# Moving a quarter of a gate's modulation from the branch merge into the linear-attention heads

## The chip, the cores and the metric

The kernel runs on one core of a Trainium2 chip. The metric is the device time of one execution in microseconds (us); the time of a kernel is the median of its runs. Five engines work side by side, each through its own instruction queue and strictly in the order of that queue: TensorE (PE in the profile; PEld is its weight load), VectorE (DVE), ScalarE (ACT), GpSimd (POOL) and SyncE (SP), which only starts transfers. An instruction that has to wait holds up everything behind it on its engine.

## The reference, cut to what matters

One layer of a diffusion backbone: 512 latent tokens and 256 context tokens, 1024 channels, float32. The conditioning vector `c` makes six modulation rows of 1024 numbers, and the one this change is about is `gt2`, the gate of the second residual:

```python
mod = jax.nn.silu(c) @ w_ada[layer] + b_ada[layer]          # w_ada: 1024 x 6144
sh1, sc1, gt1, sh2, sc2, gt2 = jnp.split(mod[:, None, :], 6, axis=-1)
h = modulate(rms_norm(x_lat, norm1_g), sh1, sc1)
# token sub-layer: latent attention (8 heads) and gated linear attention (4 heads), then
g_mla, g_gla = jnp.split(sigmoid(gate_logits), 2, axis=-1)
mix = (g_mla * br_mla + g_gla * br_gla) @ w_out
x_lat = x_lat + gt1 * mix
h = modulate(rms_norm(x_lat, norm2_g), sh2, sc2)
val, gate = split(h @ w_up)                                  # 2 x 2816 channels
x_lat = x_lat + gt2 * ((gelu(conv3x3(gate)) * val) @ w_down)
return rms_norm(x_lat, final_g)
```

`gt2` depends only on `c` and on 4 MB of `w_ada`, so it can be made at any time before it is first used, at the end of the second sub-layer. The same holds of `gt1`, `sh2` and `sc2` with their own columns of `w_ada`.

## The kernel before, in words

Every large product is done as three products in a rounded format (fp32r): each float32 operand is split into a high part and a low remainder, and hi·hi, hi·lo and lo·hi are summed in PSUM. For weights, ACT casts the high part (`whi`, or `s` where it goes into the large pool), and POOL or DVE subtracts it from the raw tile for the low part (`wlo`, or `s`). So each 512 KB of weights costs one SP transfer, one ACT cast and one subtraction before PE can use it. Raw tiles have three buffers, and SP starts the next transfer when the subtraction has freed one.

The stages, with their place in the span of the profiled execution: input normalisation and latents (0 to about 85 us), latent attention (to about 205), four heads of gated linear attention (`states`, `output`, `decay`, `apply`, `to_tokens`, called in the loop over `h` in lines 1316 to 1340; to about 409), the branch merge (loop over `j` in lines 1383 to 1425; 409 to 475), the output projection `w_out_norm` (475 to 526), the up projection with the convolution (to about 788), the down projection and the final norm.

**The heads.** In the pass over head `h`, the decay factors of head `h + 1` are made (`decay`, line 1137): ACT takes exponentials, DVE takes running sums, first for the context (tiles `C`), then for the latents (tiles `T`). Then half the merge gates of the other branch (`merge_mla`) and the next keys and queries are projected, `apply` multiplies them by the decay factors on DVE, and `to_tokens` turns the result on PE. Heads follow each other with a period of 45 us in the trace.

**The merge.** For each of eight blocks `j` of 128 channels PE makes a gate (`gb`, 24 matmuls) and a branch projection (`bg`, 12 matmuls); ACT makes the sigmoid of the gate (three instructions on tile `sg`); DVE multiplies by `bg` (`sg<-pb,sg`), adds the other branch (`sg<-sg,s`); ACT casts the high part (`s<-sg`), DVE subtracts the low part (`s<-sg,s`). These are the left operands of the output projection. Beside this, blocks 0 to 3 make `gt1` (`mod_part`, eight multiply-adds on DVE each into a PSUM tile, `p<-xn,csilu,p`), blocks 1, 2, 3 and 5 load and split four of the eight row blocks of `w_out`, and blocks 5 and 6 make two parts of `gt2`. In block 6 ACT copies the sums of `gt1` (`xn<-p`, the high part) and DVE subtracts (`xn<-p,xn`, the low part); PE then sums both over the partitions (`p<-xn,one_r`). After the merge the last four row blocks of `w_out` are cast on ACT (`s<-raw`), and their low parts go to POOL (blocks 4 and 6) and DVE (5 and 7).

**A part of `gt2`.** `gate_part(j, pool)` (line 1098) makes 256 of its 1024 columns: SP loads two tiles `wa` of 512 KB (two buffers), and DVE runs eight multiply-adds of 128x256 into tile `gt2` (`gt<-wa,csilu,gt`), four for each load. Until it is summed over the partitions, in the up projection, `gt2` is used by nobody. Before the change parts 0 and 1 are made in the pass over the last head and parts 2 and 3 in blocks 5 and 6 of the merge.

**The last weights.** The hidden channels of the last four blocks are not in the pairs of the down projection; their weights (`last`, four tiles of `w_down`) are multiplied by `gt2` on DVE and split (lines 1629 to 1637). The code asks for one of them after each of the pairs 1 to 4.

**What sets the order.** A scheduler in the build orders each engine's queue from a simulated timeline; the order of the code is a priority, `tc.issue_after(x)` keeps an instruction behind `x` in that simulated order, and only true dependences become waits on the chip. So DVE runs what the scheduler expected to be ready, and waits if on the chip it isn't. Nearly all instructions are recorded through one helper, so the profile gives lines 89 and 90 for them; the tiles tell them apart.

Of the kernel before, what the change touches and what calls it, by code (L numbers as in the profile page):

```python
# [13 lines left out]
ALU = mybir.AluOpType  # L14
# [58 lines left out]
def block_kernel(ctx: ExitStack, tc: tile.TileContext, p, out):  # L73
# [61 lines left out]
    def tt(eng, out_, a, b, op):  # L135
        return eng.tensor_tensor(out=out_, in0=a, in1=b, op=op)
# [4 lines left out]
    def split(hi, lo, src, eng=None):  # L141

        A.copy(hi, src)
        sub(eng or G, lo, src, f(hi))
# [962 lines left out]
    with tc.tile_pool(name="egl", bufs=1) as eg:  # L1107
# [208 lines left out]
        for h in range(GH):  # L1316
            St = states(h, dec)
            on = output(h, dec, Q, St)
            if h + 1 < GH:
                dec = decay(h + 1)  # L1320
                merge_mla(2 * h)
                kq = proj_kq(h + 1)
                with tc.issue_after(key_end[0].ins):
                    mod_end()
            else:
                merge_mla(2 * h)
                mod_end()
                mod_begin(S4f)
                with tc.issue_after(load[0].ins):
                    gate_part(0, eg)  # L1330
                merge_mla(2 * h + 1)
                with tc.issue_after(load[0].ins):
                    gate_part(1, eg)
            gate_out(h, on, gr)
            if h + 1 < GH:
                Q = apply(kq, dec)
                gr = gate(h + 1)
                to_tokens(dec, Q)
                mod_begin(S4f)
                merge_mla(2 * h + 1)  # L1340

    behind.clear()

# [29 lines left out]
    with tc.tile_pool(name="emg", bufs=1) as em_:  # L1373
        def merge_weights(j):
            return (split_w(load_cols(w_in, CGB + j * 128)), split_w(load_cols(w_brg, j * 128, k1=4), 512))

        def mraw():
            return tl(em_, [128, 1024], F32, "xn", 3)


        gsum = p2()
        ahead = merge_weights(0)
        for j in range(8):
            wgb, wbg = ahead
            gb = pb()
            proj(wgb, gb)
            if j + 1 < 8:
                ahead = merge_weights(j + 1)
            bg = pb()
            for k in range(4):  # L1390
                bg_ = mm3(bg, k3(wbg[0], 4, 128)[:, k, :], k3(wbg[1], 4, 128)[:, k, :], yT[k][:, 0, :], yT[k][:, 1, :], k == 0,
                    k == 3)
            sg = tl(em_, [128, 512], F32, "sg", 2)
            si = sigmoid(sg, gb)
            tt(V, sg, bg, sg, ALU.mult)
            tt(V, sg, sg, m1[j // 2][:, j % 2, :], ALU.add)
            mg[j] = S4([128, 2, 512])
            split(mg[j][:, 0, :], mg[j][:, 1, :], sg, V)
            ahead_ = load[0].ins
            if j in (1, 2, 3, 5):  # L1400
                load_wo(len(wo), mraw)
            if j == 0:
                mod_end()
            with tc.issue_after(ahead_):
                if j < 4:
                    mod_part(2048 + j * 256, gsum[:, j * 256:j * 256 + 256], mraw)
                elif j == 4:
                    mod_begin(mraw, p2()[:, 0:256])
            if j == 6:
                m_, gh, gl = mp_tile(), *[tl(em_, [128, 1024], F32R, "xn", 3) for _ in range(2)]  # L1410
                with tc.issue_after(si.ins):
                    A.copy(m_, begun[7])
                    A.copy(gh, gsum)
                sub(V, gl, gsum, f(gh))
            elif j == 7:
                with tc.issue_after(bg_.ins):
                    mod_fin(7, m_)
                    gp = p2()
                    for half in range(2):
                        hs = slice(half * 512, (half + 1) * 512)  # L1420
                        total(gp[:, hs], gh[:, hs], gl[:, hs])
                        tt(V, gt1[:, hs], gt1[:, hs], gp[:, hs], ALU.add)
            if j in (5, 6):
                with tc.issue_after(load[0].ins):
                    gate_part(j - 3, em_)
        for k in range(4, 8):
            load_wo(k)
        h2h = [S4([128, 2, 512]) for _ in range(4)]
        h2l = [S4([128, 2, 512]) for _ in range(4)]
        def w_out_norm(t):  # L1430
            cs = slice(t * 128, (t + 1) * 128)
            mp = p2()
            for k in range(8):
                for half in range(2):
                    hs = slice(half * 512, (half + 1) * 512)
                    mm3(mp[:, hs], mg[k][:, 0, cs], mg[k][:, 1, cs], wo[k][0][:, hs], wo[k][1][:, hs], k == 0, k == 7)
            xn = mraw()
            for half in range(2):
                hs = slice(half * 512, (half + 1) * 512)
                tt(V, xn[:, hs], mp[:, hs], gt1[:, hs], ALU.mult)  # L1440
                tt(V, x2[t][:, hs], x2[t][:, hs], xn[:, hs], ALU.add)
            s2 = sm(1, "s2")
            A.activation(xn, x2[t], AF.Square, accum_out=s2)
            A.dma_start(out=x2_[t], in_=x2[t])
            r2 = rstd_exp(s2, 1, 1.0 / D)
            V.tensor_scalar(out=xn, in0=x2[t], scalar1=r2, scalar2=None, op0=ALU.mult)
            return xn

        def transposed(t, xn):
            cs = slice(t * 128, (t + 1) * 128)  # L1450
            for kk in range(2):
                tp = pb()
                for k in range(4):
                    PE.transpose(tp[:, k * 128:(k + 1) * 128], xn[:, (4 * kk + k) * 128:(4 * kk + k + 1) * 128], ident)
                ht = tl(em_, [128, 4, 128], F32, "ht2", 2)
                for k in range(4):
                    kt = 4 * kk + k
                    V.tensor_scalar(out=ht[:, k, :], in0=tp[:, k * 128:(k + 1) * 128], scalar1=modsc2[:, kt:kt + 1],
                                    scalar2=modsh2[:, kt:kt + 1], op0=ALU.mult, op1=ALU.add)
                for k in range(2):  # L1460
                    split(h2h[2 * kk + k][:, :, cs], h2l[2 * kk + k][:, :, cs], ht[:, 2 * k:2 * k + 2, :], V)


        n0 = w_out_norm(0)
        n1 = w_out_norm(1)
        transposed(0, n0)
        n0 = w_out_norm(2)
        transposed(1, n1)
        n1 = w_out_norm(3)
        w0 = [up_weights(i) for i in range(2)]  # L1470
        z0 = p2()
        ps0 = [(z0[:, 0:512], z0[:, 512:1024]), (pb(), pb())]
        up_mm(w0[0], ps0[0], 0, 256)
        transposed(2, n0)
        up_mm(w0[1], ps0[1], 0, 256)
        transposed(3, n1)
        w0.append([])
        for c0 in (FF + 256, 256):
            h_, l_ = S4([128, 1024]), S4([128, 1024])
            split(h_, l_, load_cols(w_up, c0))  # L1480
            w0[2].append((h_, l_))
        z0 = p2()
        ps0.append((z0[:, 0:512], z0[:, 512:1024]))
        up_mm(w0[2], ps0[2], 0, 256)
        for i in range(3):
            up_mm(w0[i], ps0[i], 256, 512)
# [6 lines left out]
    with tc.tile_pool(name="eff", bufs=1) as ef:  # L1493
# [122 lines left out]
        for n in range(NP):  # L1616
            r = raw_()
            SY.dma_start(out=r[:, 0:512], in_=w_down[:, 2 * n, 0:512])
            SY.dma_start(out=r[:, 512:1024], in_=sums_[n][:, 1536:2048])
            wa = split_w(r, eng=G if n < 2 else V)  # L1620
            r = raw_()
            SY.dma_start(out=r, in_=sums_[n][:, 0:1024])
            wb = split_w(r, eng=G if n < 2 else V)
            a, z = n == 0, n == NP - 1
            product(p1, first[n], 0, wa, 0, a, z)
            product(p6, first[n], 768, wa, 512, a, z)
            product(p7, first[n], 512, wb, 512, a, z)
            product(p5, first[n], 256, wb, 0, a, z)
            if n == 0:
                for k in range(NF - NL, NF):  # L1630
                    last.append(S4f())
                    load[0] = SY.dma_start(out=last[-1], in_=w_down[:, k, :])
            elif n < 5:
                with tc.issue_after(done[0].ins):
                    tt(V, last[n - 1], last[n - 1], gt2, ALU.mult)
                    wl_.append((S4([128, 1024]), S4([128, 1024])))
                    split(*wl_[-1], last[n - 1], V)
            if n == NP - 3:
                bw.append(back_weights(0))
        u1, u2, u7, c22 = halves(S4f()), halves(S4f()), halves(S4f()), halves(S4f())  # L1640
# [143 lines left out]
```

## Time and profile before

| what | before |
|---|---|
| time, median of 3 runs | 889.96 us (887.29 to 890.98) |
| time of the profiled execution | 888.12 us |
| its span, from first to last instruction | 885.9 us |
| granted PE clock, mean | 0.998 |
| PE busy in the four heads and the merge, 228 to 474 us | without a wait over 0.2 us |
| period of heads 1 to 3 | 44.96, 44.96, 45.02 us |
| merge: time of one block of 36 matmuls on PE | 8.16 us |
| DMA busy share, 455 to 461 us / 478 to 486 us | 1.02 / 0.01 |
| DVE busy, 455 to 474.6 us | 17.75 of 19.6 us |

Rows of the timeline give the start in us, the duration in us (from the first start to the last end where equal neighbours are merged), engine, line, operation, tile written <- tiles read, shape and number; in square brackets the idle time of the engine before the row and what ended it. Waits are listed as "engine tile line <- what it waited for: us in total, times, longest".

### The profile page before, as it was taken

The numbers are of one execution on the slowest core, as the hardware profiler recorded it, in microseconds if no ns is written. First come the engines' busy times: TensorE is split into PE (matmuls) and PEld (weight loads), VectorE is DVE, ScalarE is ACT, GpSimd is POOL, SyncE is SP. The second block draws the span as 40 slices with busy tenths as digits, with TensorE's granted clock in tenths as the row PEclk, the third lists the DMA queues.
The fourth block names the chain that finished last, engine by engine and source line by source line (L and its number), as shares of the span: only waits on it lengthen the run. The fifth ranks groups of instructions, "written<-read, shape, count | busy, mean of one in ns | idle before, by whom it ended". The sixth has DMA issues, their size and how long they took to land.

```text
span 885.9 us, 12813 instructions
## 1 busy us (share of the span) xinstructions
PE 866.9 (98%) x4794; PEld 737.0 (83%) x4794; DVE 647.1 (73%) x1049; ACT 412.6 (47%) x666; POOL 383.8 (43%) x258
## 2 busy tenths in 40 slices
PE   7999999999999999999998999999999999999996
PEld 6788899888888888888886889888888888878885
DVE  5477788875978686986678584986677666787856
ACT  4355766773454545444544332433334333365414
POOL 2512355450534342433653521777767776500004
PEclk9999999999999999999999999999999999999999
DMA  9970001217414242637982730656556755578602
GB/s 293 319 182 1 1 4 33 73 33 206 107 37 131 61 131 60 187 87 227 280 264 96 231 102 15 225 170 198 176 168 191 211 174 182 170 276 271 213 13 95
DMA packets 141648, 130.53 MB, mean 147 GB/s; under 512 B 7947, under 2 KB 122995, under 8 KB 141586
## 3 DMA queue, kind: packets, MB, share of 16 engines
q1 hardware_dynamic: 140354, 126.67, 46.9%
q10 hardware_dynamic: 832, 2.40, 0.7%
q8 instruction: 37, 0.61, 0.3%
q0 software_dynamic: 400, 0.65, 0.3%
q14 instruction: 25, 0.20, 0.1%
HBM read 115.87 MB, written 13.63 MB: 146 GB/s over the span
## 4 chain that ended last, share of the span: by engine, by line
PE 81%; DMA 7%; issue 4%; DVE 4%; POOL 2%; ACT 2%; SPq 0%; POOLq 0%; DVEq 0%; ACTq 0%
PE pb L90 41%; PE p L90 20%; PE pb L89 14%; PE p L89 6%; DMA raw<-in_w_ada_dram 3%; DMA raw<-in_w_br_gla_dram 2%; POOL wlo L90 1%; POOL s L90 1%; DVE s L90 1%; DMA s<-in_w_down_dram 1%; DMA xn<-in_w_ada_dram 1%; ACT P L90 1%; DVE mx L90 1%; DVE kT L90 0%; DMA xn<-in_w_out_dram 0%
## 5 line engine op out<-in xcount | busy, mean ns | idle before, releaser
L90 POOL TENSOR_TENSOR wlo<-raw,whi 128x1024 fp32r<-128x1024 f32 (+1 forms) x91 | 210.0, 2315 | 219.4 <-ACT whi L90 188.9
L90 PE MATMUL pb<-s,whi 128*128 128x512 f32 (+1 forms) x906 | 271.3, 382 | 0.0
L90 PEld LDWEIGHTS pb<-s,whi 128*128 128x128 f32 x906 | 167.3, 188 | 32.3
L90 PE MATMUL pb<-s,wlo 128*128 128x512 f32 (+1 forms) x453 | 172.7, 381 | 0.0
L90 ACT CAST whi<-raw 128x1024 fp32r<-128x1024 f32 (+1 forms) x106 | 102.9, 975 | 120.1 <-PE pb L90 47.4
L90 DVE SCALAR_TENSOR_TENSOR ac<-pb,cwT,ac 128x441 f32<-128x441 f32 (+2 forms) x160 | 110.9, 694 | 13.5 <-ACT ac L90 9.2
L89 PE MATMUL pb<-s,whi 128*128 128x512 f32 x320 | 101.2, 394 | 0.0
L90 PEld LDWEIGHTS pb<-s,wlo 128*128 128x128 f32 x453 | 85.2, 188 | 16.3
L90 PE MATMUL p<-s,s 128*128 128x512 f32 (+1 forms) x398 | 84.3, 364 | 2.4 <-POOL s L90 1.9
L90 PEld LDWEIGHTS p<-s,s 128*128 128x128 f32 x398 | 66.9, 189 | 15.1 <-POOL s L90 2.2
L89 PEld LDWEIGHTS pb<-s,whi 128*128 128x128 f32 x320 | 59.3, 188 | 11.5
L89 PE MATMUL pb<-s,wlo 128*128 128x512 f32 x160 | 62.8, 392 | 0.0
L90 PE MATMUL p<-whi,s 128*128 128x512 f32 x168 | 55.8, 393 | 0.0
L90 PE MATMUL pb<-whi,s 128*128 128x512 f32 x164 | 53.2, 390 | 0.0
L90 POOL TENSOR_TENSOR s<-s,edge 128x512 f32<-128x512 f32 x7 | 10.5, 1508 | 93.8 <-ACT s L90 93.8
L90 ACT ACTIVATE ac<-ac 128x512 f32<-128x512 f32 x22 | 13.9, 632 | 75.9 <-DVE ac L90 75.9
L90 PE MATMUL pb<-s,s 128*32 128x128 f32 (+2 forms) x340 | 46.1, 319 | 0.2 <-DVE rv L90 0.2
L90 DVE TENSOR_TENSOR pl<-pb,ph 128x512 fp32r<-128x512 f32 x48 | 33.0, 687 | 13.0 <-ACT ph L90 12.5
L90 PE MATMUL p<-kT,s 128*128 128x512 f32 (+1 forms) x192 | 41.2, 350 | 0.9 <-ACT P L90 0.9
L90 PEld LDWEIGHTS pb<-s,s 128*128 128x128 f32 (+1 forms) x340 | 36.1, 159 | 6.1 <-issue 0.7
L90 PE MATMUL p<-s,whi 128*128 128x256 f32 (+1 forms) x156 | 38.6, 338 | 0.0
L90 ACT CAST ph<-pb 128x512 fp32r<-128x512 f32 x48 | 28.2, 587 | 20.7 <-PE pb L90 20.5
(274 smaller groups left out, 1672.2 us busy)
## 6 DMA issues: line engine op xcount, KB each, us to landing
raw<-in_w_up_dram SPq DMA_DIRECT2D x44, 512.0 KB, 5.1
raw<-in_w_in_dram SPq DMA_DIRECT2D x28, 512.0 KB, 4.3
rawd<-in_w_down_dram SPq DMA_DIRECT2D x22, 512.0 KB, 5.2
s<-in_w_ada_dram SPq DMA_DIRECT2D x20, 512.0 KB, 6.8
ws<-rawd SPq DMA_DIRECT2D x18, 512.0 KB, 5.7
raw<-in_w_ada_dram SPq DMA_DIRECT2D x10, 512.0 KB, 7.5
xn<-in_w_ada_dram SPq DMA_DIRECT2D x10, 512.0 KB, 5.1
wa<-in_w_ada_dram SPq DMA_DIRECT2D x8, 512.0 KB, 5.7
```

Source lines behind the costliest of these rows:

```text
L89: return fn(*args, **kw)
L90: ins = fn(*args, **kw)
```

## The change

Parts of `gt2` change their place, and the code asks for the scaling of the last weights after other pairs. Nothing is computed differently.

```diff
             else:
                 merge_mla(2 * h)
                 mod_end()
                 mod_begin(S4f)
                 with tc.issue_after(load[0].ins):
-                    gate_part(0, eg)
+                    gate_part(1, eg)
                 merge_mla(2 * h + 1)
                 with tc.issue_after(load[0].ins):
-                    gate_part(1, eg)
+                    gate_part(2, eg)
             gate_out(h, on, gr)
             if h + 1 < GH:
...
                 mod_begin(S4f)
                 merge_mla(2 * h + 1)
+                if h == 1:
+                    with tc.issue_after(load[0].ins):
+                        gate_part(0, eg)
...
-            if j in (5, 6):
+            if j == 6:
                 with tc.issue_after(load[0].ins):
-                    gate_part(j - 3, em_)
+                    gate_part(3, em_)
...
-            elif n < 5:
+            elif n in (1, 2, 4, 5):
+                r = last[len(wl_)]
                 with tc.issue_after(done[0].ins):
-                    tt(V, last[n - 1], last[n - 1], gt2, ALU.mult)
+                    tt(V, r, r, gt2, ALU.mult)
                     wl_.append((S4([128, 1024]), S4([128, 1024])))
-                    split(*wl_[-1], last[n - 1], V)
+                    split(*wl_[-1], r, V)
```

What the scheduler makes of it, at three places. The first is DVE in the pass over head 1, where the decay factors for head 2 are made (`C` context, `T` latents); the changed kernel has:

```order
L90 TENSOR_TENSOR C_521_3170<-C_521_3170,C_520_3169 128x512
L90 SCALAR_TENSOR_TENSOR gt_404_2389<-wa_3492,csilu_78,gt_404_2389 128x256
L90 SCALAR_TENSOR_TENSOR C_520_3169<-ones_74,C_521_3170 128x256 x2
L90 SCALAR_TENSOR_TENSOR gt_404_2389<-wa_3492,csilu_78,gt_404_2389 128x256
L90 TENSOR_SCALAR C_521_3170<-C_520_3169 128x256 x2
L90 SCALAR_TENSOR_TENSOR gt_404_2389<-wa_3492,csilu_78,gt_404_2389 128x256 x2
L90 TENSOR_SCALAR T_519_3168<-p_515_3164,pcol_72 128x512
L90 SCALAR_TENSOR_TENSOR gt_404_2389<-wa_3498,csilu_78,gt_404_2389 128x256 x3
L90 TENSOR_SCALAR T_519_3168<-p_515_3164,pcol_72 128x512
L90 SCALAR_TENSOR_TENSOR gt_404_2389<-wa_3498,csilu_78,gt_404_2389 128x256
L90 TENSOR_REDUCE so_3152<-w_510_3150 128x4
```

The eight `gt` rows are new there and stand between rows that were neighbours before; the first of each four waits for its `wa` load. On SP the two `wa` loads stand right behind the load of `w_br_mla` for that pass. On ACT one exponential of `C` has moved behind the first `T<-p`. PE and POOL keep their order.

The second place is DVE in blocks 5 to 7 of the merge. Before, the sums of part 2 (`wa_4606`, `wa_4612`) and part 3 (`wa_4683`, `wa_4689`) stood between the rows of blocks 5 (`sg_4591`) and 6 (`sg_4668`):

```order
L90 SCALAR_TENSOR_TENSOR gt_404_2389<-wa_4606,csilu_78,gt_404_2389 128x256 x3
L90 SCALAR_TENSOR_TENSOR gt_404_2389<-wa_4612,csilu_78,gt_404_2389 128x256 x4
L90 TENSOR_TENSOR sg_4591<-pb_4578,sg_4591 128x512
L90 SCALAR_TENSOR_TENSOR gt_404_2389<-wa_4683,csilu_78,gt_404_2389 128x256
L90 TENSOR_TENSOR sg_4591<-sg_4591,s_594_3657 128x512
L90 SCALAR_TENSOR_TENSOR gt_404_2389<-wa_4683,csilu_78,gt_404_2389 128x256 x2
L90 TENSOR_TENSOR s_772_4597<-sg_4591,s_772_4597 128x512
L90 SCALAR_TENSOR_TENSOR gt_404_2389<-wa_4683,csilu_78,gt_404_2389 128x256
L90 SCALAR_TENSOR_TENSOR gt_404_2389<-wa_4689,csilu_78,gt_404_2389 128x256 x4
L90 TENSOR_TENSOR sg_4668<-pb_4655,sg_4668 128x512
L90 TENSOR_TENSOR xn_4679<-p_685_4149,xn_4678 128x1024
```

and now (block 5 is `sg_4603`):

```order
L90 SCALAR_TENSOR_TENSOR gt_404_2389<-wa_4683,csilu_78,gt_404_2389 128x256 x4
L90 SCALAR_TENSOR_TENSOR gt_404_2389<-wa_4689,csilu_78,gt_404_2389 128x256 x3
L90 TENSOR_TENSOR sg_4603<-pb_4590,sg_4603 128x512
L90 SCALAR_TENSOR_TENSOR gt_404_2389<-wa_4689,csilu_78,gt_404_2389 128x256
L90 TENSOR_TENSOR sg_4603<-sg_4603,s_596_3669 128x512
L90 TENSOR_TENSOR s_774_4609<-sg_4603,s_774_4609 128x512
L90 TENSOR_TENSOR sg_4668<-pb_4655,sg_4668 128x512
L90 TENSOR_TENSOR xn_4679<-p_687_4161,xn_4678 128x1024
```

Eight sums are gone, and the remaining eight take the place that part 2 had. On SP the pair of `wa` loads now stands behind the last `w_br_gla` load instead of ahead of it, and the four `w_out` loads that follow have no `wa` load between them.

The third place is DVE at the start of the down projection, where `gt_404_2389` scales the last weights. Before:

```order
L90 TENSOR_TENSOR s_1130_7189<-s_1130_7189,gt_404_2389 128x1024
L90 TENSOR_TENSOR s_1140_7234<-s_1129_7187,s_1139_7233 128x1024
L90 TENSOR_TENSOR s_1131_7191<-s_1131_7191,gt_404_2389 128x1024
L90 TENSOR_TENSOR wlo_7283<-raw_7279,whi_7282 128x1024
L90 TENSOR_TENSOR wlo_7289<-raw_7286,whi_7288 128x1024
L90 TENSOR_TENSOR s_1132_7193<-s_1132_7193,gt_404_2389 128x1024
L90 TENSOR_TENSOR s_1148_7276<-s_1130_7189,s_1147_7275 128x1024
L90 TENSOR_TENSOR wlo_7325<-rawd_7321,whi_7324 128x1024
L90 TENSOR_TENSOR s_1156_7318<-s_1131_7191,s_1155_7317 128x1024
```

and now:

```order
L90 TENSOR_TENSOR s_1130_7189<-s_1130_7189,gt_404_2389 128x1024
L90 TENSOR_TENSOR s_1140_7234<-s_1129_7187,s_1139_7233 128x1024
L90 TENSOR_TENSOR s_1131_7191<-s_1131_7191,gt_404_2389 128x1024
L90 TENSOR_TENSOR wlo_7283<-raw_7279,whi_7282 128x1024
L90 TENSOR_TENSOR wlo_7289<-raw_7286,whi_7288 128x1024
L90 TENSOR_TENSOR s_1132_7193<-s_1132_7193,gt_404_2389 128x1024
L90 TENSOR_TENSOR s_1148_7276<-s_1130_7189,s_1147_7275 128x1024
L90 TENSOR_TENSOR wlo_7320<-rawd_7316,whi_7319 128x1024
L90 TENSOR_TENSOR s_1162_7355<-s_1131_7191,s_1161_7354 128x1024
```

Only the numbers of tiles differ. From the end of the merge on, every engine's queue holds the same operations in the same order as before.

## The prediction

> **What bounds the kernel now.** I read the shares of the engines first, then the list of what PE waited for in the two stages that the change touches, then the timeline around the waits found.
>
> ```profile
> PE 866.9 (98%) x4794; PEld 737.0 (83%) x4794; DVE 647.1 (73%) x1049; ACT 412.6 (47%) x666; POOL 383.8 (43%) x258
> PE p L90 <- POOL s L90: 1.9, 1, 1.9
> PE p L90 <- DVE xn L90: 1.8, 1, 1.8
> PE p L89 <- DVE C L90: 0.2, 1, 0.2
> ```
>
> PE sets the end: 98% of the span. The last three rows are everything that PE waited for from 228 to 520 us, heads, merge and output projection together. So work that comes off DVE, or goes onto it, counts only through PE's waits, and here there are two to win, 3.65 us together. They lie where the merge ends:
>
> ```profile
> 477.23 0.50 PE L90 MATMUL p<-xn,one_r 128*128 128x512 f32 x1 [1.78 <-DVE xn L90]
> 485.79 20.29 PE L90 MATMUL p<-s,s 128*128 128x512 f32 x88 [1.87 <-POOL s L90]
> ```
>
> PE could have gone on at 475.45 and at 483.92. First it lacks the low part of gt1's sums (DVE's `xn`), then the low part of w_out's row block 4 (POOL's `s`). Without the first wait it would be at the second place at 482.14. DVE over the same time:
>
> ```profile
> 461.03 1.65 DVE L90 SCALAR_TENSOR_TENSOR gt<-wa,csilu,gt 128x256 f32<-128x256 f32 x1 [0.80 <-DMA wa<-in_w_ada_dram]
> 463.00 4.51 DVE L90 SCALAR_TENSOR_TENSOR gt<-wa,csilu,gt 128x256 f32<-128x256 f32 x7
> 467.42 0.68 DVE L90 TENSOR_TENSOR sg<-pb,sg 128x512 f32<-128x512 f32 x1
> 471.53 3.91 DVE L90 SCALAR_TENSOR_TENSOR gt<-wa,csilu,gt 128x256 f32<-128x256 f32 x4 [0.19 <-DMA wa<-in_w_ada_dram]
> 475.36 0.68 DVE L90 TENSOR_TENSOR sg<-pb,sg 128x512 f32<-128x512 f32 x1
> 475.96 1.22 DVE L90 TENSOR_TENSOR xn<-p,xn 128x1024 fp32r<-128x1024 f32 x1
> 477.09 0.68 DVE L90 TENSOR_TENSOR sg<-sg,s 128x512 f32<-128x512 f32 x1
> 480.28 0.69 DVE L90 TENSOR_TENSOR sg<-pb,sg 128x512 f32<-128x512 f32 x1 [1.13 <-ACT sg L90]
> ```
>
> The `sg<-pb` rows at 467.42, 475.36 and 480.28 are blocks 5, 6 and 7. DVE runs late because 16 sums of `gt2` stand between them. ACT is late with it, since its queue alternates with DVE's:
>
> ```profile
> 469.45 0.62 ACT L90 CAST s<-sg 128x512 fp32r<-128x512 f32 x1 [5.35 <-DVE sg L90]
> 470.93 0.59 ACT L90 ACTIVATE sg<-pb 128x512 f32<-128x512 f32 x1
> 471.55 1.30 ACT L90 ACTIVATE sg<-sg 128x512 f32<-128x512 f32 x2
> 473.01 1.02 ACT L90 CAST xn<-p 128x1024 fp32r<-128x1024 f32 x1
> 477.80 0.62 ACT L90 CAST s<-sg 128x512 fp32r<-128x512 f32 x1 [3.77 <-DVE sg L90]
> 478.33 0.59 ACT L90 ACTIVATE sg<-pb 128x512 f32<-128x512 f32 x1
> 482.26 2.94 ACT L90 CAST s<-raw 128x1024 fp32r<-128x1024 f32 x3
> 483.38 5.70 POOL L90 TENSOR_TENSOR s<-raw,s 128x1024 fp32r<-128x1024 f32 x2 [9.79 <-ACT s L90]
> ```
>
> The cast for block 5 (469.45) waited for DVE; the sigmoid of block 6 stands behind it and ends at 472.85. The cast for block 6 (477.80) again waited for DVE, and behind it stand the sigmoid of block 7, its cast, and at 482.26 the casts of the w_out rows, from which POOL's subtraction and PE's second wait follow. From 477.80 on this is one chain of engines handing on; no transfer ends a wait in it.
>
> **The change, part by part: the merge.** Eight of the 16 sums and the second pair of loads go. The rest takes the place of the first pair.
>
> ```profile
> 454.71 0.98 SPq L90 DMA_DIRECT2D wa<-in_w_ada_dram  x2
> 456.09 0.42 SPq L90 DMA_DIRECT2D raw<-in_w_br_gla_dram  x1
> DMA to landing us min/median/max: 3.8/5.7/7.3
> L90 DVE SCALAR_TENSOR_TENSOR gt<-wa,csilu,gt 128x256 f32<-128x256 f32 x16 | 11.7, 730 | 1.6 <-DMA wa<-in_w_ada_dram 1.2
> L90 DVE SCALAR_TENSOR_TENSOR p<-xn,csilu,p 128x256 f32<-128x256 f32 x14 | 6.8, 486 | 0.3
> ```
>
> The third row is for the eight `wa` loads of the whole kernel, the last two for the merge from 450 to 480 us. The pair now goes out behind the w_br_gla load, at 456.09 + 0.42 = 456.5; after the median 5.7 us DVE can begin at 462.2. Seven sums stand ahead of block 5. They cost 3.4 us at 486 ns (what the `p` sums took beside them), 5.1 us at 730 ns; I take the 4.5 us that seven took at 463.00. Then `sg<-pb` (0.6 us from start to start), the eighth sum (0.4) and `sg<-sg` (0.6): 462.2 + 4.5 + 1.6 = 468.3, so ACT's cast of block 5 comes 1.1 us before 469.45, and the sigmoid of block 6 and the high part of gt1 with it: 474.03 - 1.1 = 472.9. Nothing now stands before DVE's `xn`; it runs from 472.9 to 474.1, before PE is there at 475.45. **The first wait goes: -1.78.**
>
> `sg<-sg` of block 6 follows at 474.1 and ends at 474.8, where it ended at 477.78: 3.0 us earlier. The chain moves with it, POOL's block 4 from 485.79 to 482.8, while PE is there at 482.14. So 1.2 us of the second wait goes. With sums at 486 ns the chain moves by more than 3.65 us and all 1.87 goes; between the two I take 1.5. **Second wait: -1.5.** The other end: loads landing after 7.3 us and sums at 730 ns put the cast of block 5 at 470.5, 1.0 us later than before. `xn` then ends at 476.3 instead of 477.18, the first wait keeps 0.9, and the chain gains 0.9 in all. So the merge is worth between -0.9 and -3.65 us, and I take -3.3. The last w_out row block, loaded once DVE has freed a buffer, hangs on the casts at 482.26 and moves with them.
>
> **The heads.** Two loads and eight sums are added in the pass over head 1, in the middle of the decay chain, and what is queued behind them is the `T` chain, which feeds ACT's exponentials, `apply`, and PE's turns.
>
> ```profile
> 298.56 0.37 SPq L89 DMA_DIRECT2D raw<-in_w_br_mla_dram  x1
> 302.76 1.27 DVE L90 TENSOR_TENSOR_SCAN C<-ones,C 128x256 f32<-128x256 f32 x2
> 305.88 0.75 DVE L90 TENSOR_SCALAR T<-p,pcol 128x512 f32<-128x512 f32 x1 [1.33 <-ACT T L90]
> 307.40 0.75 DVE L90 TENSOR_SCALAR T<-p,pcol 128x512 f32<-128x512 f32 x1 [0.77 <-ACT T L90]
> 308.97 0.69 DVE L90 TENSOR_REDUCE so<-w 128x4 f32<-128x512 f32 x1 [0.82 <-ACT w L90]
> 321.75 1.72 DVE L90 TENSOR_TENSOR T<-gk,T 128x1024 f32<-128x1024 f32 x1 [2.43 <-ACT gk L90]
> 325.35 0.75 DVE L90 SCALAR_TENSOR_TENSOR gr<-pb,pcol,gr 128x512 f32<-128x512 f32 x1 [0.34 <-PE pb L89]
> 326.02 2.93 DVE L90 TENSOR_TENSOR s<-T,ml 128x1024 f32<-128x1024 f32 x1
> 331.33 0.82 PE L89 MATMUL p<-cst,s 128*128 128x128 f32 x6
> ```
>
> The loads go out at 298.93. The next pass shows the same pair in the same place on SP, and when it landed:
>
> ```profile
> 360.50 1.05 SPq L89 DMA_DIRECT2D wa<-in_w_ada_dram  x2
> 365.12 3.94 DVE L90 SCALAR_TENSOR_TENSOR gt<-wa,csilu,gt 128x256 f32<-128x256 f32 x4 [0.84 <-DMA wa<-in_w_ada_dram]
> 332.15 7.98 PE pb L89 x35
> 377.17 7.95 PE pb L89 x35
> ```
>
> 4.6 us, so 303.5, and DVE waits 0.8 us at 302.76. The sums cost 3.9 us at 486 ns, 5.8 at 730. DVE's idle times at 305.88, 307.40 and 308.97 swallow 2.9. So the `T` chain is 1.8 to 3.7 us late. What may be late: `T<-gk,T` ends at 323.47 and the next row but small ones waits for PE until 325.35, 1.9 us; `s<-T,ml` ends at 328.95 and PE turns it at 331.33, 2.4 us: 4.3 together. **Cost: 0.** The next pass bears it out: there eight sums stood ahead of and behind `T<-gk,T`, and PE's repeated piece came 45.02 us after the one before, which is the undisturbed period within 0.1 us. If the cover were gone it would cost up to 3.7.
>
> [...]
>
> **The last weights.** Tile numbers apart, DVE's queue there is the same row by row, and so are all others. This half does nothing: 0.
>
> **Sum.** -1.78 - 1.5 + 0 = -3.3 us. The profiled execution took 888.12 us, 2.2 more than its span of 885.9; it becomes 884.8. Behind 485.79 PE is dense up to 769 us, so the gain is kept. The runs' median stands 1.8 us above the profiled execution, so I put **886.7 us**, 0.37% less. A half per cent, 4.4 us, is about what can be told from no change, since three runs spread over 3.7; the whole gain to be had, 3.65, is below it.
>
> **The rivals.**
>
> *The first sums stay late.* Loads landing after 7.3 us and slow sums keep most of the chain: 0.9 to 2 us gained, 888.4. For it: the merge's transfers already end waits (0.80 at 461.03). Against it: nothing else is loaded then that was not before, and 1 MB fewer follows.
>
> *The wait moves.* PE, arriving earlier, waits for w_out's later rows or the up weights instead: 1.8 gained, 888.2. Against it: their buffers are freed by the same chain that moves.
>
> *Nothing comes of it.* PE's waits are refilled by an equal wait, for instance for block 7's `sg`, and the time stays at 890.0. Against it: DVE waited 1.13 us at 480.28 for a sigmoid that only stood behind block 6's cast.
>
> *Slower: the head's loads block DVE.* Place: DVE's queue at 302.76. If the pair lands after 7.3 us (306.2; DVE waits 3.5) and each sum takes the 1.65 us of the one at 461.03, the `T` chain is 3.5 + 13.2 - 2.9 = 13.8 us late, 9.5 beyond the cover, and the kernel stands at 889.96 + 9.5 - 3.3 = 896.2. It decides from a lateness of 4.3 + 3.3 = 7.6 us. Against it: the next pass had the loads after 4.6 us and the four sums at 365.12 took 3.94.
>
> **How the numbers follow.** Forecast 0.60, first sums late 0.18, the wait moves 0.08, nothing 0.09, slower 0.05. The forecast's own range is 885.2 to 888.2, from the caps of the sum and a spread of a us between medians. The range that leaves out two in ten is 884.6 to 890.3. Faster by over 0.5% means under 885.5: a quarter of the forecast's 0.60 by that spread, and little else, 0.17. Slower means over 894.4: 0.04. Within: 0.79.
>
> **What would show it.** In the changed profile PE's wait for `xn` is gone, and that for POOL's `s` is under 0.7 us; DVE's `xn` starts at the end of ACT's cast of `xn`, near 473; ACT's first `s<-raw` starts between 478.2 and 479.3; the period of head 2 is within 0.1 us of 44.96; no `gt` row waits for DMA over 1.5 us. A PE wait for `s` near 331, or a first `gt` row of the merge after 463.5, would make the prediction wrong.

## The result and the profile after

The changed kernel took 885.21 us (median of 13 runs), the kernel before 889.66 us beside it: a ratio of 0.9957, interval 0.9938 to 0.9977, which is 2.0 to 5.5 us less, 3.8 in the middle. One of the 13 runs took 1081.01 us at a granted clock of 0.752 and is not in the ratio. The forecast was 886.7 us with a range from 884.6 to 890.3, and "within half a per cent". The profiled execution took 884.84 us with a span of 882.9; the sum of the prediction had put it at 884.8.

PE's list of waits from 228 to 520 us, the same view that the prediction began with, and the place in PE's timeline where the two waits had stood:

```profile
PE p L90 <- POOL s L90: 0.6, 1, 0.6
PE p L89 <- DVE C L90: 0.2, 1, 0.2
474.92 0.71 PE L90 MATMUL p<-xn,one_r 128*128 128x512 f32 x2
475.46 5.60 PE L90 MATMUL p<-s,s 128*128 128x512 f32 x24
482.37 7.79 PE L90 MATMUL p<-s,s 128*128 128x512 f32 x33 [0.61 <-POOL s L90]
```

The wait for `xn` is gone: the two products with it stand in one row, without a gap. The wait for POOL's `s` is 0.61 us instead of 1.87. PE is past this place at 482.37, where it was at 485.79. The waits explain 1.78 + 1.26 = 3.04 of these 3.42 us. DVE, ACT and POOL over the same time:

```profile
460.81 5.41 DVE L90 SCALAR_TENSOR_TENSOR gt<-wa,csilu,gt 128x256 f32<-128x256 f32 x7 [0.56 <-DMA wa<-in_w_ada_dram]
466.13 0.68 DVE L90 TENSOR_TENSOR sg<-pb,sg 128x512 f32<-128x512 f32 x1
471.26 0.69 DVE L90 TENSOR_TENSOR sg<-pb,sg 128x512 f32<-128x512 f32 x1 [2.08 <-ACT sg L90]
472.49 1.22 DVE L90 TENSOR_TENSOR xn<-p,xn 128x1024 fp32r<-128x1024 f32 x1 [0.54 <-ACT xn L90]
467.84 0.62 ACT L90 CAST s<-sg 128x512 fp32r<-128x512 f32 x1 [6.09 <-DVE sg L90]
478.81 2.94 ACT L90 CAST s<-raw 128x1024 fp32r<-128x1024 f32 x3
459.49 3.83 POOL L90 TENSOR_TENSOR wlo<-raw,whi 128x1024 fp32r<-128x1024 f32 x2 [2.97 <-ACT whi L90]
```

The cast of block 5 starts at 467.84 instead of 469.45, `xn` at 472.49 instead of 475.96, the casts of w_out's rows at 478.81 instead of 482.26. In block 6 DVE now waits for ACT (2.08, 0.54). Before, these two rows (475.36, 475.96) came without a wait, and ACT waited 3.77 us for DVE's block 6 (477.80); now it waits 1.95.

In the heads the added sums stand in the `T` chain, and PE takes its turns as before:

```profile
302.95 0.48 DVE L90 SCALAR_TENSOR_TENSOR gt<-wa,csilu,gt 128x256 f32<-128x256 f32 x1 [0.32 <-DMA wa<-in_w_ada_dram]
308.05 2.71 DVE L90 SCALAR_TENSOR_TENSOR gt<-wa,csilu,gt 128x256 f32<-128x256 f32 x1
308.06 2.41 POOL L90 TENSOR_TENSOR wlo<-raw,whi 128x1024 fp32r<-128x1024 f32 x1 [9.55 <-PE pb L89]
323.84 1.72 DVE L90 TENSOR_TENSOR T<-gk,T 128x1024 f32<-128x1024 f32 x1 [2.43 <-ACT gk L90]
326.21 1.59 DVE L90 TENSOR_TENSOR s<-T,ml 128x1024 f32<-128x1024 f32 x1
331.31 0.82 PE L89 MATMUL p<-cst,s 128*128 128x128 f32 x6
287.17 7.98 PE pb L89 x35
332.12 7.98 PE pb L89 x35
```

`T<-gk,T` starts 2.1 us later than before (321.75), the turns at 331.31 as before (331.33). The last two rows are from the chain of waits: a period of 44.95 us, 44.96 before.

Not all of the 3.42 us is left at the end: the span is 3.0 shorter. In this profile 0.3 of it is in the last wait before the down projection, which was 0.57 us for `wlo` at 788.02 before:

```profile
784.88 0.50 PE L90 MATMUL p<-wlo,s 128*128 128x512 f32 x1 [0.87 <-DVE wlo L90]
```

In the second profile of the changed kernel (experiment 5) this wait was 0.55 us, so that the 0.3 us are a fixed price of the change is not shown.

### The profile page after: what moved, and what is told of

Same layout as the page of the kernel before. It is cut to its first block, busy times and chain, and to the rows that moved or that the text cites. A ratio compares the mean times of both kernels' runs of the same rounds, so it can differ in the third digit from the quotient of the medians.

```text
span 882.9 us, 12813 instructions
## 1 busy us (share of the span) xinstructions
PE 866.2 (98%) x4794; PEld 737.3 (83%) x4794; DVE 645.3 (73%) x1049; ACT 413.5 (47%) x666; POOL 385.3 (44%) x258
## 4 chain that ended last, share of the span: by engine, by line
PE 86%; DVE 3%; DMA 3%; issue 3%; POOL 2%; ACT 2%; SPq 0%; POOLq 0%; DVEq 0%; ACTq 0%
PE pb L90 46%; PE p L90 20%; PE pb L89 14%; PE p L89 6%; DMA raw<-in_w_ada_dram 2%; POOL wlo L90 1%; DVE s L90 1%; POOL s L90 1%; DMA s<-in_w_down_dram 1%; ACT P L90 1%; DVE mx L90 1%; DVE kT L90 0%; ACT ph L90 0%; ACT s L90 0%; DVE P L90 0%
```

## The experiments

Each was timed beside the kernel before. "Merge" is PE's waits in the merge and the output projection, "234" a wait that the prediction doesn't speak of, near 234 us, where PE takes the products of the modulation sums `mp`. It is in some executions and not in others, in kernels that are the same there, and moves a span by 1.8 to 5.3 us, as much as what is looked for. So the experiments are read by the waits first, and by the times only where the interval allows it.

| kernel | median us (runs) | ratio, interval | profiled span | merge | 234 |
|---|---|---|---|---|---|
| before | 889.66 (13) | 1 | 885.9 | 3.65 | 0 |
| the change | 885.21 (13) | 0.9957 (0.9938 to 0.9977) | 882.9 | 0.61 | 0 |
| 1, loads kept, six sums out | 889.25 (12) | 0.9973 (0.9952 to 0.9993) | 889.8 | 1.87 | 1.93 |
| 2, eight sums twice | 887.96 (12) | 0.9973 (0.9947 to 0.9999) | 885.9 | 1.91 | 0 |
| 3, part 2 left out | 887.36 (12) | 0.9944 (0.9924 to 0.9965) | 885.7 | 0 | 1.90 |
| 4, the scaling alone | 891.05 (12) | 0.9992 (0.9973 to 1.0011) | 889.7 | 3.44 | 1.85 |
| 5, the change again | 883.82 (10) | 0.9948 (0.9930 to 0.9965) | 883.7 | 0.26 | 0 |
| 6, no part in the merge | 885.37 (12) | 0.9958 (0.9942 to 0.9974) | 882.7 | 0 | 0 |
| 7, two parts in one head | 884.87 (12) | 0.9963 (0.9944 to 0.9983) | 882.2 | 0.38 | 0 |
| 8, as 6, and VectorE for POOL | 883.34 (6) | 0.9946 (0.9924 to 0.9967) | 880.7 | 0 | 0 |
| 9, the change, and VectorE for POOL | 885.02 (8) | 0.9948 (0.9930 to 0.9967) | 883.9 | 0.52 | 0 |
| 10, as 8 once more | 884.02 (6) | 0.9939 (0.9922 to 0.9956) | 882.3 | 0 | 0 |

The kernel before had medians of 890.84 beside 1 to 4, 888.47 beside 5 to 8, 889.11 beside 9 and 10.

**1 and 2: the sums, or the loads?** From the kernel before, six of the second gate's 16 sums in the merge are left out, and all loads stay in their places:

```diff
-            for k in range(4):
+            for k in range(1 if j == 2 else 4):
                 V.scalar_tensor_tensor(out=acc, in0=r3[:, k, :], ...
```

> The kernel before, with both of the merge's gate parts and all four of their loads in their old places, but only the first of the four sums of each load of part 2 (six sums are left out, so that gt2 is wrong). Theory A (VectorE's sums hold the chain): PE's wait for xn, 1.78 us before, is gone, the wait for POOL's s is 0.6 us or less instead of 1.87, and the kernel gains 3.0 to 3.6 us of span, as the change did. Theory B (the second pair of loads, 1 MB, holds w_out's rows or the weights back): both waits stay within 0.5 us of 1.78 and 1.87, and the span within 0.5 us of 885.9.

The wait for `xn` is gone, as theory A had it; that for `s` is still 1.87 us, as theory B had it. The timelines of DVE and SP show why:

```profile
468.38 0.48 DVE L90 SCALAR_TENSOR_TENSOR gt<-wa,csilu,gt 128x256 f32<-128x256 f32 x1 [0.20 <-DMA wa<-in_w_ada_dram]
472.25 2.83 DVE L90 SCALAR_TENSOR_TENSOR gt<-wa,csilu,gt 128x256 f32<-128x256 f32 x2 [2.05 <-DMA wa<-in_w_ada_dram]
467.81 1.45 SPq L90 DMA_DIRECT2D wa<-in_w_ada_dram  x2
489.03 1.48 PE L90 MATMUL p<-s,s 128*128 128x512 f32 x3 [1.87 <-POOL s L90]
```

The second pair of loads goes out only when the first pair's tiles have been read (467.81), lands 4.4 us later, and DVE stands 2.05 us with the rest of its queue behind. Before, sums filled this time. So the second pair holds the chain too, not by its bytes but by its buffers. (Ten sums are left here, two more than in the changed kernel, since each load of part 2 keeps one.)

The other way round, from the changed kernel, the last part's eight sums twice on the same two loads:

```diff
-            for k in range(4):
+            for k in (range(4) if j < 3 else (0, 1, 2, 3, 0, 1, 2, 3)):
                 V.scalar_tensor_tensor(out=acc, in0=r3[:, k, :], ...
```

> The changed kernel, in which the eight sums of part 3 in the merge are done twice on the same two loads (the second eight add a term that does not belong there): 16 sums and two loads in the merge. Theory A (sums): both waits come back, 2.0 to 3.6 us together, since only the second pair's transfers are spared (0.2 to 0.4 us of DVE's waits) and the first pair's begin is 0.2 us earlier; span 884.2 to 885.9. Theory B (loads): as the changed kernel, 0.6 us of waits and a span of 882.9.

```profile
468.30 5.12 DVE L90 SCALAR_TENSOR_TENSOR gt<-wa,csilu,gt 128x256 f32<-128x256 f32 x6
475.06 0.68 DVE L90 TENSOR_TENSOR sg<-sg,s 128x512 f32<-128x512 f32 x1
483.77 6.45 PE L90 MATMUL p<-s,s 128*128 128x512 f32 x20 [1.91 <-POOL s L90]
```

Six of the sums take 5.12 us; block 6's `sg<-sg` comes at 475.06, in the changed kernel at 473.64. PE's second wait is back, 1.91 us, the first is not: below the 2.0 to 3.6 of theory A and far from the 0.6 of B. In this execution DVE was 0.95 us ahead when it came to block 4 (456.17 against 457.12), and without that head start the waits would have been inside A's bounds; that is argued, not shown. Together: eight more sums on the old loads, and the second pair of loads with two more sums, each bring back the wait for `s` (1.91 and 1.87); neither brings back the one for `xn`. That one needed both. In experiment 1 PE came to this place 5.2 us late, because of the wait near 234 and the half clock behind it, so the chain is better measured from PE's last products with `mp`: the casts of w_out's rows start 7.65 us behind them in the kernel before (474.61 to 482.26), 5.69 in experiment 1 (479.81 to 485.50), 5.59 in experiment 2 (474.65 to 480.24) and 4.26 in the changed kernel (474.55 to 478.81). Each half alone wins about 2.0 of the 3.4 us.

**3: the head's price from the other side.** From the kernel before, part 2 is dropped from the merge and put nowhere.

```diff
-            if j in (5, 6):
+            if j == 6:
                 with tc.issue_after(load[0].ins):
                     gate_part(j - 3, em_)
```

> The kernel before with part 2 of the gate left out of the merge and put nowhere (a quarter of gt2 keeps the bias alone), so with the changed kernel's merge and without its added load on head 2. If the head's eight sums cost nothing, as forecast: span 882.9 within 0.3 us, PE's waits in heads and merge 0.8 us, as in the changed kernel. If the sums in the head cost something that the list of waits hides: a span lower than the changed kernel's by that price, up to 3.7 us (879.2).

Between 245 us and the end of the merge nothing is left but the 0.2 us for `C`, in the heads as in the changed kernel; the wait for `s` is 0, where 0.6 had been expected. The span of 885.7 is no answer, since this execution has the wait of 1.90 us near 234; the ratio of 0.9944 overlaps with the change's. The price of the head is read from the changed kernel's rows above: no wait, the same period.

**4: the scaling alone.**

```diff
-            elif n < 5:
+            elif n in (1, 2, 4, 5):
+                r = last[len(wl_)]
...
```

> The kernel before with only the second half of the change (the last weights' scaling at pairs 1, 2, 4, 5 instead of 1 to 4). Forecast: no difference, span 885.9 within 0.4 us and the ratio's interval holding 1, since every engine's queue is the same row by row. Rival (the half that was costed at nothing is part of the gain): a span below 885.4 with the same 3.65 us of waits in the merge.

The ratio is 0.9992, its interval holds 1: no effect. The span of 889.7 missed the expectation, not by the edit but by two things in this execution that the first profile of the kernel before does not have. PE's timeline at the end of the merge, and the windows behind it (length, then busy time of PE, PEld, DVE, ACT, POOL; the granted clock is the third number from the right):

```profile
480.81 0.54 PE L90 MATMUL p<-xn,one_r 128*128 128x512 f32 x1 [2.65 <-DVE xn L90]
481.15 7.24 PE L90 MATMUL p<-s,s 128*128 128x512 f32 x24
481.00:484.00 3.00, 3.00 (x8) 2.38 (x8) 1.19 (x3) 2.38 (x4) 0.00 (x0) 0.52 0.02 5
```

The waits of the merge are spread otherwise here: 2.65 us for `xn` and three of 0.33 and less. After the wait for `xn` PE ran at half clock: the 24 products that took 5.65 us in the first profile took 7.24. So this wait cost 1.6 us beyond its length. The other thing is the wait near 234, below.

**5: the change again**, unedited.

> The changed kernel once more, as the measure for the three runs beside it. Theory (the merge's two waits are worth 3.0 us, and two things beside them move single executions: VectorE and POOL start within 0.05 us of each other at 233.9, and when POOL is first PE waits 1.9 us for mp and then runs at half clock for about 3.4 us): PE's waits from 228 to 520 us are 0.8 us and the span 882.9 without that wait, 886.0 with it; the ratio to the kernel before between 0.993 and 0.997. Rival (the change's gain hangs on something that differs from execution to execution): a merge with over 1.5 us of waits, or a ratio above 0.998.

The ratio is 0.9948, the merge has 0.26 us of waits, there is no wait near 234. The span of 883.7 carries 1.1 us from the kernel's first 225 us, where the change has nothing (the products with `mp` come at 235.62 instead of 234.51).

**6: does the last part still cost?** Part 3 goes to the pass over head 0.

```diff
-                if h == 1:
+                if h < 2:
                     with tc.issue_after(load[0].ins):
-                        gate_part(0, eg)
+                        gate_part(3 * h, eg)
...
-            if j == 6:
-                with tc.issue_after(load[0].ins):
-                    gate_part(3, em_)
```

> The changed kernel with part 3, the last one in the merge, moved to the pass over head 0 in the same way as part 0 to the pass over head 1: no sums and no loads of the second gate in the merge. Theory A (what is left of the wait for POOL's s, 0.61 us, still hangs on VectorE's sums): the wait goes, PE waits 0 in the merge, and the kernel gains at most 0.6 us against the changed one; the head costs 0. Theory B (the rest hangs on the chain of ACT and PE): the wait stays at 0.6 and the span within 0.2 us of the changed kernel's. If head 1 now costs something, PE waits in it between 277 and 287 us, up to 3 us.

The merge has no wait left and PE starts the row block at 481.41, 0.96 us before the changed kernel: theory A. Head 1 costs nothing. But the span is only 0.2 shorter, and the ratio is the change's. PE's timeline shows where the time goes now:

```profile
743.99 0.70 PE L90 MATMUL pb<-s,whi 128*128 128x512 f32 x2 [0.28 <-DVE ac L90]
784.68 0.50 PE L90 MATMUL p<-wlo,s 128*128 128x512 f32 x1 [0.96 <-DVE wlo L90]
```

1.24 us, where before there were 0.57 and in the changed kernel 0.87. From 740 us on DVE's convolution is the slower chain (eight of its operations in 5.8 us, and with all else on it 9.58 us from one such group to the next, 757.19 to 766.77), and what PE wins in the merge it partly waits for there. How much differs between executions: with the same code behind the merge, the profile of 8 has no wait there and that of 10 has 1.1 us.

**7: how much cover does a head have?** Part 1 goes from the last head to the place of part 0.

```diff
                 if h == 1:
                     with tc.issue_after(load[0].ins):
                         gate_part(0, eg)
+                        gate_part(1, eg)
```

> The changed kernel with part 1 taken from the pass over the last head and put behind part 0 in the pass over head 1: 16 sums and four loads in one decay chain; the merge as in the changed kernel. Theory A (cover of 4.3 us, of which the changed kernel uses 2.1): the eight sums more cost 3.2 to 3.9 us, so the T chain is 5.3 to 6.0 us late and PE waits 1.0 to 1.7 us for s or T near 331, and the period of head 2 grows by as much. Theory B (the cover is longer than reckoned, since the product that PE turns took 1.59 us there instead of 2.93): lateness 5.3 to 6.0 and no wait over 0.3 us. If one more subtraction of POOL stops a sum, both are 2 us later: 3.0 to 3.7 us of wait by A, up to 2 by B.

```profile
312.36 2.39 DVE L90 TENSOR_SCALAR rv<-so 128x4 f32<-128x4 f32 x1
316.60 2.32 DVE L90 TENSOR_TENSOR_SCAN T<-s,T 128x512 f32<-128x512 bf16 x2
324.88 1.72 DVE L90 TENSOR_TENSOR T<-gk,T 128x1024 f32<-128x1024 f32 x1 [1.36 <-ACT gk L90]
331.31 0.82 PE L89 MATMUL p<-cst,s 128*128 128x128 f32 x6
```

No wait: theory B on the result. But the lateness that both theories had reckoned with (5.3 to 6.0 us) was wrong: with 16 sums `T<-gk,T` is 3.1 us later than before, 1.0 more than with eight. Two things gave time back. POOL's subtractions met other rows: in the changed kernel a sum (2.71) and the two scans (4.49 together), with 16 sums another sum (1.98, at 309.07) and a small operation (`rv`, 2.39 instead of 0.17), while the scans took 2.32. Together these rows are 0.7 us shorter, 6.69 against 7.37. And DVE's wait for `gk` before `T<-gk,T`, 2.43 us in the kernel before and in the changed one, fell to 1.36.

**8, 9 and 10: the wait near 234.** From kernel 6 (8 and 10) and from the changed kernel (9), the low parts of the first head's three weights are subtracted on VectorE:

```diff
-            wk = split_w(load_cols(w_in, CGK + h * 128))
+            wk = split_w(load_cols(w_in, CGK + h * 128), eng=V if h == 0 else None)
...
```

with the same for `wq` and `wr`. With it PE's queue takes the products with `mp` 2.4 us later.

> The kernel with no gate part in the merge, in which also the low parts of the first head's three weights (key, query, gate) are subtracted on VectorE instead of POOL. Theory (PE's wait of 1.9 us for mp near 234 comes from VectorE's sums of mp being stopped by POOL's subtractions, 2.6 us each instead of 0.5): those sums take about 0.4 us each beside the three subtractions of 1.2, the last one that PE needs ends near 232.5 instead of 233.9 or 236.2, and the wait never comes: span 882.3 in every execution, the median of the times 884.5 or less, and the spread of the times under 4 us instead of 6. Rival (the wait at 234 comes from somewhere else, the late loads for instance): the wait is found in about every second execution as before, and the spread stays.

> The changed kernel with the low parts of the first head's three weights subtracted on VectorE instead of POOL (with it the queue of PE takes the products with mp 2.4 us later, at 236.8), the merge as changed. Theory (the wait near 234 for mp, 1.9 us and half clock behind it, is found in some executions of every kernel and makes the upper half of the spread): no wait there, span 881 to 882.9, the times within 4 us of each other, the median 0 to 2 us under the changed kernel's 883.8 to 885.2. Rival: the spread of 4 to 6 us and the median stay, because single executions differ by something else.

> The kernel of the run before last of this study (no gate part in the merge, three subtractions on VectorE) once more, for more executions. Theory: no wait near 234 and none in the merge, span 880.5 to 882.5, ratio to the kernel before 0.992 to 0.995, median 882.5 to 884. Rival: the 880.7 of its first profile was chance; span 882.5 or more and a ratio like the changed kernel's.

None of the three has the wait, and the 12 times of 8 and 10 lie between 882.3 and 884.8 us; the 22 of the change in its ratios, from both its runs, between 882.3 and 889.4. But 9, which has the same edit, lies between 882.8 and 886.4 with the change's ratio of 0.9948, and three profiles without the wait don't show that it can't come. Since PE also takes the products later, they don't show either which of the two, the engine of the subtraction or the later use, keeps it away. Of the kernels that leave nothing out, 8 and 10 have the lowest ratios, 0.9946 and 0.9939; their intervals overlap with the change's, so that they are faster than the change isn't shown.

## Why the prediction was right, step by step

**The first wait, -1.78:** right, with its mechanism. `xn` was forecast from 472.9 to 474.1, ahead of PE; it ran from 472.49.

**The second wait, -1.5:** 1.26. The casts of w_out's rows were forecast between 478.2 and 479.3 and started at 478.81, PE's product at 482.8 and started at 482.37. The chain moved 3.45 us (482.26 to 478.81) instead of 3.0. What is left of the wait is larger than forecast because PE, too, was earlier than reckoned: it was ready at 482.37 - 0.61 = 481.76, not at 482.14. Two steps on the way were off and cancelled. The loads were to land at 462.2 by the median; the sums began at 460.81, since the loads went out 0.8 us earlier and landed after 5.1. And the seven sums took 5.41 us instead of the 4.5 taken. The prediction bounded them by 486 and 730 ns for each, as if a sum had a price. One by one, five took under half a microsecond and the first two, beside POOL's two subtractions (459.49, 3.83 us), 2.80 together:

```profile
460.81 1.37 DVE L90 SCALAR_TENSOR_TENSOR gt<-wa,csilu,gt 128x256 f32<-128x256 f32 x1 [0.56 <-DMA wa<-in_w_ada_dram]
462.21 1.40 DVE L90 SCALAR_TENSOR_TENSOR gt<-wa,csilu,gt 128x256 f32<-128x256 f32 x1
463.64 0.49 DVE L90 SCALAR_TENSOR_TENSOR gt<-wa,csilu,gt 128x256 f32<-128x256 f32 x1
```

The 730 ns were a mean over these two kinds: of the 16 sums of the kernel before three took 1.65, 1.40 and 2.35 us, the others 0.47 or 0.48.

**The heads, 0:** right. The `T` chain was 2.1 us late, inside the 1.8 to 3.7, and the cover of 4.3 held. Of the eight sums one was slow: that at 308.05 took 2.71 us, the others about 0.5, and a subtraction of POOL beside it started at 308.06 and took 2.41. The cover was sized too small: 16 sums found room too. And its second half was not drawn on, by luck: `s<-T,ml` had taken 2.93 us beside a subtraction of POOL (325.46, 2.41 us), which now came later (326.67). It took 1.59 us and ended at 327.80, 1.15 us earlier than before, so the lateness did not reach this product. The subtraction now lay beside the next one, `s<-gq,T`, which took 3.41 us (327.72) instead of 1.21, and PE did not wait for that. The prediction had not reckoned with either.

**The scaling, 0:** right, by experiment 4.

**That the gain is kept:** nearly. Of 3.42 us at 482.37, 2.9 to 3.0 are left at the end. The prediction saw that PE is dense up to 769 us, and did not ask what is behind DVE's 0.57 us for `wlo`, which was 0.87 here and 0.55 in experiment 5.

**The median, 886.7:** 885.21, and 883.82 in experiment 5. The profiled execution met the sum (884.84 for 884.8), so the difference lies in what one profile leaves out: it stands 0.4 us under its median, where the prediction had added 1.8. The step that was mis-sized is "the whole gain to be had, 3.65": it prices a wait by its length. The profile of before had its two waits without a fall of the clock; the same queues in experiment 4 had 3.44 us of waits and lost 1.6 more at half clock. In two profiles that is one of two; how often it happens was not measured. The last section lays the waits beside the falls of the clock that were measured; what decides whether a fall follows was not shown. Such falls can account for ratios of 0.9957 and 0.9948, 3.8 and 4.6 us, against 3.0 in the first pair of profiles, but so can chance within the intervals. Whether half a per cent was reached (885.2 by the ratio 0.995) is open for the same reason: the two ratios lie on either side.

The rivals: the first sums didn't stay late, since the loads landed after 5.1 us and not 7.3. The wait moved to another place by 0.3 us at most, and not to w_out's rows. DVE in the head waited 0.32 us for the loads, where the slow case needed 3.5.

## What to carry to other kernels

Work taken off an engine that isn't the bound is worth the bottleneck's waits that hang on it, so look for these waits and follow the chain back from them; here two waits of 3.65 us in 886 were, beside 0.2 us, all that the heads, the merge and the output projection had, and the place to put the work was a stage where the same engine stood idle or early. Before a second load is counted as bytes, ask which buffer it waits for, and before the mean of a group is taken as a price, look whether it mixes two kinds of rows. When a wait that is removed had brought the clock down, its end is worth more than its length (in experiment 2 a wait of 1.91 us cost 1.7 us more); and when a chain has been freed, the next slowest (here the convolution on VectorE) can take part of the gain.

## What the runs showed of the hardware

**After a wait of 1.91 us PE's clock was halved for 3.4 us.** This is experiment 2, and the windows show it (columns as above):

```profile
484.00:485.00 1.00, 1.00 (x5) 0.82 (x5) 1.00 (x2) 0.00 (x0) 1.00 (x1) 0.93 0.00 0
485.00:488.00 3.00, 3.00 (x8) 2.33 (x8) 0.39 (x1) 0.00 (x0) 2.03 (x1) 0.50 0.69 231
488.00:489.00 1.00, 1.00 (x5) 0.78 (x5) 0.00 (x0) 0.37 (x1) 0.00 (x0) 0.87 1.15 335
```

0.07 + 1.50 + 0.13 = 1.7 us lost, which is 3.4 us at half clock. It starts 1.1 us after the wait's end; in experiment 4, behind 2.65 us, 0.3 after it. Half clock followed waits of 1.87 us (experiment 1, in the merge), 1.90 (experiment 3) and 1.93 (experiment 1, near 234, twice as long there), and did not follow 1.78 and 1.87 us in the first profile of the kernel before and 1.85 near 234 in experiment 4. So a wait of 1.87 us was followed by half clock once, and once not: its length alone doesn't tell.

The windows of one and two microseconds give the times. With 1.00 ahead of a fall and 0.50 behind it, a granted clock of 0.83 from 236 to 237 us and of 0.63 from 489 to 490 us puts the two falls of experiment 1 at 236.67 and 489.26; in the same way the clock fell at 484.85 in 2 (0.93 in its window), at 237.07 in 3 (0.54) and at 481.13 in 4 (0.57). It was back after 3.4 us each time, but after 6.8 us behind the first fall of experiment 1. The two falls of experiment 1 are 252.59 us apart. The trace of the kernel before records the full clock from 7.745 us to the fall behind the last product at 881.557, that of the changed kernel from 7.075 to 877.473. These stretches of 873.81 and 870.40 us differ by 3.41, and the three distances are 74, 256 and 255 times 3.4133 us. So the recorded changes of the clock in these three executions lie on a grid of such steps; for experiments 2 to 4 the same step is an estimate. Laid back from the fall behind the last product, and in experiment 1 from 489.26, the grid gives PE's busy time in a step (the second number of a row), here for the two waits of the kernel before and for the second of experiment 1:

```profile
475.37:478.79 3.42, 1.64 (x8) 1.30 (x8) 2.73 (x5) 0.99 (x2) 0.00 (x0) 1.00 0.02 5
482.20:485.61 3.41, 1.72 (x8) 1.07 (x6) 2.19 (x3) 3.00 (x4) 2.23 (x1) 1.00 0.00 0
485.84:489.25 3.41, 1.54 (x7) 0.98 (x6) 2.21 (x2) 2.59 (x3) 2.63 (x2) 1.00 0.00 0
489.25:492.67 3.42, 3.42 (x9) 2.65 (x9) 1.41 (x2) 0.00 (x0) 3.03 (x1) 0.50 0.42 147
```

The falls that were measured had ahead of them, within one step of this grid, waits of 1.87 us (experiment 1, in the merge), 1.90 (3), 1.91 (2), 1.93 (1, near 234) and 2.65 (4). Behind the first 10 us and up to the last products, no step of the kernel before has PE standing for more than 1.78 us, none of the changed kernel for more than 0.94, and the granted clock of both stayed at 1.00. By the grid the 1.87 us of the kernel before were cut by the end of a step at 485.61, into 1.69 and 0.18; the 1.85 us of experiment 4 at 235.37, into 0.97 and 0.88; the 1.78 us lay in one step. So the grid agrees with all the waits listed here, but that it decides was not shown. It leaves open why the half clock of 6.8 us lasted two steps, though PE stood in neither.

**Beside POOL's subtraction, one sum of VectorE took 0.47 us in the changed kernel and 2.57 to 2.65 in experiments 1, 3 and 4, where PE came out 1.8 to 5.3 us later.** The case is the sum of `mp` that PE waits for near 234, and the subtraction of POOL beside it. In the changed kernel:

```profile
233.91 0.47 DVE L90 SCALAR_TENSOR_TENSOR mp<-s,csilu,mp 128x256 f32<-128x256 f32 x1
233.95 2.68 POOL L90 TENSOR_TENSOR wlo<-raw,whi 128x1024 fp32r<-128x1024 f32 x1 [0.25 <-ACT whi L90]
```

and in experiment 3, where the program is the same at this place:

```profile
233.60 2.62 DVE L90 SCALAR_TENSOR_TENSOR mp<-s,csilu,mp 128x256 f32<-128x256 f32 x1
233.58 2.35 POOL L90 TENSOR_TENSOR wlo<-raw,whi 128x1024 fp32r<-128x1024 f32 x1 [0.19 <-ACT whi L90]
236.27 0.61 PE L90 MATMUL pb<-ones,mp 128*128 128x1 f32 x4 [1.90 <-DVE mp L90]
237.00:240.00 3.00, 3.00 (x16) 3.00 (x16) 2.14 (x6) 0.00 (x0) 0.00 (x0) 0.51 0.67 174
```

With DVE 0.04 us ahead, POOL took 0.33 us longer (2.68 against 2.35) and PE did not wait. With POOL 0.02 us ahead, the sum took 2.62 us instead of 0.47, PE waited 1.90 and its clock was halved behind it: the end of the merge came 3.3 us later than in the changed kernel (477.89 against 474.55 for the last products with `mp`). Three of the nine profiles of kernels with this piece unchanged have the wait (1.93 us in experiment 1, 1.90 in 3, 1.85 in 4). In the first profile of the kernel before, without it, DVE was recorded 0.21 us ahead. In experiment 1, with it, DVE was recorded 0.02 ahead (233.89 against 233.91), and the sum took 2.65; the sum in the head, 0.01 us ahead at 308.05, took 2.71. So a recorded lead of 0.02 us does not tell the two outcomes apart, and that the start decides was not shown. The wait has nothing to do with the change, and it is a part of the 6 us and more by which single executions of one kernel differ (885.65 to 893.21 us in the kernel before). In experiment 4 the same wait, without the fall of the clock, put PE 1.8 us behind; in experiment 1, with a longer one, 5.3 (479.81).
